# Ordering every engine's work by the program text in the merge stage of a hybrid attention/GLA step

## The chip, the cores and the metric

The kernel runs on one core of one Trainium2 chip. The metric is the device time of one execution, in microseconds, as the median of several runs. TensorE (PE in the profile) multiplies, VectorE (DVE), ScalarE (ACT) and GpSimd (POOL) work on tiles, and SyncE (SP) issues the transfers of the stage that this document is about.

## The reference

One inference step over 2048 new prompt tokens and 64 sample tokens (2112 in all), model width 1024. Sliding-window attention and gated linear attention (GLA) run beside each other; their outputs are projected, gated per channel, added, projected again and normalised with the residual. The part that matters here is the end:

```python
h_att = jnp.einsum('bta,ad->btd', o_att * jax.nn.silu(g_att), w_pa)
h_gla = jnp.einsum('btv,vd->btd', o_gla * jax.nn.silu(g_gla), w_pg)
merged = jax.nn.sigmoid(r_att) * h_att + jax.nn.sigmoid(r_gla) * h_gla
y = jnp.einsum('btd,de->bte', merged, w_o)
x = layer_norm(DN_ALPHA * x + y, ln_g, ln_b)
```

`r_att` and `r_gla` are projections of x (weights `w_ra` and `w_rg`), so there are four large products of the tokens with a weight matrix, then one with `w_o`. Everything is float32.

## The kernel before

**Stages.** First the attention over six token chunks, then the GLA over four heads times six chunks, then the merge (lines 970 to 1144), then the output projection with the normalisation (line 1149 on). All of it is one program without loops on the chip.

**Precision.** Each float32 operand is split in two parts: `split` (lines 111 to 114) copies it on ACT with rounding (`xh`, `wh`) and takes the rest on DVE (`xl`, `wl`). A product is three matmuls: hi*hi, hi*lo, lo*hi (lines 1141 to 1143).

**The merge.** It has four *passes*: pass 0 with `w_pa` on the attention's output, pass 1 with `w_ra` on x, pass 2 with `w_rg` on x, pass 3 with `w_pg` on the GLA's output. Each pass multiplies in blocks by a Strassen-like scheme with seven products, in the *steps* 1, 2, 7, 6, 5, 3, 4 (`ORDER`). Each step runs over three token parts (`MS`), so a pass has 21 *units* (n, counted from 0 to 83), and each unit has four *groups*, one for each output block p. A group is 6 matmuls in pass 0 and 12 in the others, of 352 columns each, into one PSUM bank. There are five such banks (`pa`), and a group can start when the bank of the group five before it has been read.

**What follows a group.** `combine` reads the bank. Steps 1 and 7 copy it with ACT (lines 1025 and 1031). Step 6 adds on DVE (L1034) and then on POOL (L1035). Steps 2, 5, 3 and 4 complete an output block: they add on DVE (L1028, L1038 with L1039, L1042, L1045) and call the pass's *sink*. Pass 0 stores the block (L1051). Pass 1 takes a tanh on ACT (L1054), a multiply with a loaded block `cs` on DVE (L1055), and stores (L1056). Pass 2 takes a tanh on ACT (L1059) and stores (L1060). Pass 3 multiplies with a loaded block on DVE (L1063), adds another on POOL (L1064) and stores (L1065).

**What goes ahead of a unit.** The input block of unit n+2 (n+3 in pass 0) is loaded (L1001), that of unit n+1 is split, the raw weight tiles `ws` of a later step are loaded (L975), added on POOL for the steps that need sums (lines 982 to 988), and split into `wh` and `wl`. The weights of a step are made over the three units before it: two blocks in the first, one in each of the other two. There are two buffers for split inputs, so the input of unit n+1 can be split only when PE has finished unit n-1. The blocks `cs` are loaded four groups ahead into eight buffers. Blocks that end in the `fin` tile (steps 2 and 5) share six buffers.

**Besides.** In pass 2 the last six *input sums* (`combine_x`, loads L831 and L832, POOL lines 834 to 837, stores L839) prepare inputs for pass 3. In pass 3 four of the eight tiles of `w_o` are loaded (L1105) and split, for the stage behind the merge.

**What sets the order.** PE's instructions run in the order of the text throughout (a `manual_schedule` region for PE). For the other engines and SP's queue of transfers a planner places each instruction, by its own estimate of when it can start and with text order as priority. An engine executes its queue in that order: an instruction that waits holds up all behind it. The planner can thus put an instruction far ahead of its place in the text; in this kernel the first `w_o` load, which the text has in unit 64, stands in SP's queue while PE is in unit 33.

Of the kernel before, what the change touches and what calls it, by code (L numbers as in the profile page):

```python
# [51 lines left out]
def kernel(ctx, tc, io):  # L52
# [773 lines left out]

    def combine_x(new):
# [9 lines left out]
        nc.gpsimd.tensor_tensor(x2[:, t0], x1[:, t0], x2[:, t0], ALU.subtract)  # L837
        for n_, x_, t in ((0, x1, t1), (1, x1, t0), (2, x2, t1), (3, x2, t0)):
            nc.sync.dma_start(dst[n_, :, s, k], x_[:, t])  # L839

    def chain(B):
# [117 lines left out]
    def toks(s, t):  # L959
        return slice((2 * s + t) * T, (2 * s + t + 1) * T)  # L960

    class Pass:

        def __init__(self, w, kh, src, kept, parts, sink):
            self.w, self.kh, self.src, self.kept, self.parts, self.sink = w, kh, src, kept, parts, sink
            self.A, self.acc = {}, {}
# [9 lines left out]

        def prep_w(self, i, p, r):
            A, tt = self.A, nc.gpsimd.tensor_tensor  # L980
            if i == 7:
                tt(r[0], r[0], r[1], ALU.subtract)
# [6 lines left out]
            a = A[p, "s2"] if i == 6 else A.pop((p, "s1")) if i == 5 else r[0]  # L989
# [30 lines left out]
        def combine(self, i, p, s, ps, parts):  # L1020
# [25 lines left out]
            if z is not None:  # L1046
                c, t = FINAL[i]
                self.sink(z, parts, 2 * p + c, toks(s, t))

    def store_sink(z, parts, ct, ts):  # L1050
        nc.sync.dma_start(ha_d[:, ct, ts], z)  # L1051

    def gated_sink(z, parts, ct, ts):
        nc.scalar.activation(z, z, AF.Tanh, scale=0.5)  # L1054
        nc.vector.scalar_tensor_tensor(z, z, 1.0, parts[0], ALU.add, ALU.mult)  # L1055
        nc.sync.dma_start(ta_d[:, ct, ts], z)  # L1056

    def gate_sink(z, parts, ct, ts):
        nc.scalar.activation(z, z, AF.Tanh, scale=0.5)  # L1059
        nc.sync.dma_start(tg_d[:, ct, ts], z)  # L1060

    def merge_sink(z, parts, ct, ts):
        nc.vector.scalar_tensor_tensor(z, parts[0], 1.0, z, ALU.add, ALU.mult)  # L1063
        nc.gpsimd.tensor_tensor(z, z, parts[1], ALU.add)  # L1064
        nc.sync.dma_start(mg_d[:, ct, ts], z)  # L1065

# [35 lines left out]

    def wo_load(pool, i, bufs):
        st = pool.tile([P, D], F32, tag="wst", name="wst", bufs=2)
        nc.sync.dma_start(st, io["w_o"][i])  # L1105
        hi, lo = (pool.tile([P, D], F32R, tag="wo", name=n, bufs=bufs) for n in ("woh", "wol"))
# [10 lines left out]
    issue_x(2)  # L1117
    make_x(0)
    make_w(-1)
    issue_w(0)  # L1120
    wo = []
    for n, (q, i, s) in enumerate(units):
        if n >= 2 * len(ORDER) * MS and n % 3 == 0 and combos:
            combine_x(lambda t: mtile("xc", 2 * T, 5))
        if n >= 3 * len(ORDER) * MS and n % 4 == 0 and len(wo) < 4:
            wo.append(wo_load(mo, len(wo), 8))
        issue_x(n + 3 if q.kh == 2 else n + 2)
        issue_w(n + 1)
        make_x(n + 1)
        make_w(n)  # L1130
        xh, xl = xp.pop(n)
        for p in range(NP4):
# [6 lines left out]
            for k in range(q.kh):  # L1139
# [3 lines left out]
                mm(ps, wl[:, ks], xh[:, ts], start=False, stop=(k == q.kh - 1))  # L1143
            q.combine(i, p, s, ps, parts.get(g))
    phase.close()
# [5 lines left out]
    for i in range(len(wo), 8):  # L1151
        wo.append(wo_load(sb, i, 8))
    wo = [wo[:4], wo[4:]]
# [162 lines left out]
```

## Time and profile before

| | |
|---|---|
| median of 3 runs | 1909.57 us (1908.79 to 1911.14) |
| the profiled execution | 1904.76 us |
| its span, first to last instruction | 1902.9 us |
| PE busy | 1819.0 us, 96% |
| DVE, ACT, POOL busy | 1243.9, 847.8, 518.2 us |
| granted clock of PE, mean | 0.983 |
| merge, first to last matmul | 1095.87 to 1687.70 us |

The profile is one execution; times in it are microseconds from the span's first instruction. "L1055" is line 1055 of the kernel. A row of the timeline has start, duration, engine, line, operation, what it writes and reads, and in brackets how long its engine was idle before it and what ended that. A row of a group has `xcount | total busy, mean ns | idle before it`, with the releasers. A row of the waits has the total, the number and the longest.

### The profile page before, as it was taken

Reading aid. Unit: us, or ns where it says so; the run is one execution under the profiler, and the core shown is the slowest. Engines: PE = TensorE matmul, PEld = TensorE weight load, DVE = VectorE, ACT = ScalarE, POOL = GpSimd, SP = SyncE. Lnnn points to the kernel's source line nnn. Section 1 sums busy time; section 2 is a strip of 40 time slices with the busy share of each in tenths; the row PEclk is TensorE's granted clock in tenths of the full one; section 3 lists DMA queues with packets and bytes.
Section 4 is the critical chain, followed back from the end, with each engine's and each line's share of the span. In section 5 each row is a group of like instructions: output and inputs, shape, how many; then the busy total and the mean of one; then the engine's idle time right before and its main releaser. Section 6 shows DMA issues by size and latency. Waiting matters only on the chain.

```text
span 1902.9 us, 32427 instructions
## 1 busy us (share of the span) xinstructions
PE 1819.0 (96%) x11683; PEld 1725.1 (91%) x11683; DVE 1243.9 (65%) x2552; ACT 847.8 (45%) x1942; POOL 518.2 (27%) x667
## 2 busy tenths in 40 slices
PE   6999999999999999999999799997999999979997
PEld 5988998889999999999999799997999999967886
DVE  4587768755675666557655559648746655956665
ACT  3444546545664664556555453434553543221100
POOL 3310111422134114213321133552322154621121
PEclk8999999999999999999999999998999999989999
DMA  6211012543365236424722289878975866884441
GB/s 223 89 38 41 25 45 86 157 144 115 106 216 179 84 122 227 146 81 147 227 79 61 78 278 309 284 268 297 322 238 169 261 216 214 272 296 168 137 138 60
DMA packets 200929, 316.03 MB, mean 166 GB/s; under 512 B 21720, under 2 KB 162864, under 8 KB 200752
## 3 DMA queue, kind: packets, MB, share of 16 engines
q1 hardware_dynamic: 195520, 307.70, 49.5%
q0 software_dynamic: 5248, 6.26, 1.2%
q8 instruction: 92, 1.51, 0.3%
q14 instruction: 69, 0.57, 0.1%
HBM read 228.72 MB, written 86.14 MB: 165 GB/s over the span
## 4 chain that ended last, share of the span: by engine, by line
PE 77%; DMA 8%; DVE 5%; POOL 4%; ACT 3%; issue 2%; SPq 1%; POOLq 0%; DVEq 0%; ACTq 0%
PE pd L180 9%; PE pd L181 9%; PE pd L182 9%; PE pa L1142 7%; PE pa L1141 7%; PE pa L1143 7%; PE pd L193 6%; PE pd L195 6%; PE pd L194 6%; PE pa L401 2%; DMA wst<-w_o 1%; DMA cs<-tg_d 1%; PE pa L386 1%; PE pa L731 1%; PE pa L732 1%
## 5 line engine op out<-in xcount | busy, mean ns | idle before, releaser
L180 PE MATMUL pd<-x,wh 128*128 128x384 f32 (+2 forms) x1248 | 409.6, 328 | 8.4 <-ACT x L113 5.3
L182 PE MATMUL pd<-x,wl 128*128 128x384 f32 (+2 forms) x1248 | 403.6, 323 | 1.3 <-DVE wl L114 1.3
L181 PE MATMUL pd<-x,wh 128*128 128x384 f32 (+2 forms) x1248 | 403.8, 324 | 0.9 <-DVE x L114 0.9
L1141 PE MATMUL pa<-xh,wh 128*128 128x352 f32 x1176 | 382.7, 325 | 17.7 <-DVE a L1034 9.7
L1142 PE MATMUL pa<-xl,wh 128*128 128x352 f32 x1176 | 380.6, 324 | 7.6 <-DVE xl L114 7.3
L1143 PE MATMUL pa<-xh,wl 128*128 128x352 f32 x1176 | 379.8, 323 | 0.0
L180 PEld LDWEIGHTS pd<-x,wh 128*128 128x128 f32 x1248 | 236.8, 190 | 17.8 <-issue 8.1
L1141 PEld LDWEIGHTS pa<-xh,wh 128*128 128x128 f32 x1176 | 222.2, 189 | 19.6 <-DVE a L1034 10.0
L181 PEld LDWEIGHTS pd<-x,wh 128*128 128x128 f32 x1248 | 236.8, 190 | 2.3 <-DVE x L114 2.1
L182 PEld LDWEIGHTS pd<-x,wl 128*128 128x128 f32 x1248 | 236.3, 189 | 1.9 <-DVE wl L114 1.9
L1142 PEld LDWEIGHTS pa<-xl,wh 128*128 128x128 f32 x1176 | 223.2, 190 | 11.9 <-DVE xl L114 11.8
L1143 PEld LDWEIGHTS pa<-xh,wl 128*128 128x128 f32 x1176 | 221.9, 189 | 0.0
L114 DVE TENSOR_TENSOR xl<-xs,xh 128x1408 fp32r<-128x1408 f32 x63 | 108.0, 1714 | 75.9 <-ACT xh L113 61.8
L113 ACT CAST x<-xst 128x384 fp32r<-128x384 f32 (+3 forms) x164 | 77.9, 485 | 160.2 <-PE pd L194 121.4
L193 PE MATMUL pd<-wh,x 128*128 128x256 f32 x512 | 148.0, 289 | 0.0
L194 PE MATMUL pd<-wh,x 128*128 128x256 f32 x512 | 144.9, 283 | 0.3 <-POOL x L114 0.2
L195 PE MATMUL pd<-wl,x 128*128 128x256 f32 x512 | 144.6, 282 | 0.0
L113 ACT CAST xh<-xs 128x1408 fp32r<-128x1408 f32 x63 | 86.4, 1372 | 99.5 <-PE pa L1143 75.4
L723 POOL TENSOR_SCALAR sq<-sq 128x1 f32<-128x1 f32 (+1 forms) x68 | 17.8, 262 | 375.3 <-ACT ring L722 375.3
L193 PE MATMUL pd<-woh,x 128*128 128x512 f32 x256 | 101.8, 398 | 13.2 <-ACT x L113 9.8
L194 PE MATMUL pd<-woh,x 128*128 128x512 f32 x256 | 101.3, 396 | 0.9 <-DVE x L114 0.9
L195 PE MATMUL pd<-wol,x 128*128 128x512 f32 x256 | 101.3, 396 | 0.6 <-DVE wol L114 0.5
(310 smaller groups left out, 3753.1 us busy)
## 6 DMA issues: line engine op xcount, KB each, us to landing
wst<-wt SPq DMA_DIRECT2D x33, 512.0 KB, 3.6
xs<-xc_d SPq DMA_DIRECT2D x24, 704.0 KB, 5.5
u<-xT SPq DMA_DIRECT2D x84, 192.0 KB, 3.9
xst<-xT SPq DMA_DIRECT2D x76, 192.0 KB, 2.7
xs<-xT SPq DMA_DIRECT2D x18, 704.0 KB, 6.1
ws<-w_ra SPq DMA_DIRECT2D x36, 256.0 KB, 4.7
ws<-w_rg SPq DMA_DIRECT2D x36, 256.0 KB, 5.1
ws<-w_pg SPq DMA_DIRECT2D x36, 256.0 KB, 3.9
```

The costliest lines, as they stand in the source:

```text
L113: nc.scalar.copy(dst_h, src)
L114: eng.tensor_tensor(dst_l, src, dst_h.bitcast(F32), ALU.subtract)
L180: mm(ps, hi[:, s], xh[:, :T], start=(k == 0), stop=False)
L181: mm(ps, hi[:, s], xl[:, :T], start=False, stop=False)
L182: mm(ps, lo[:, s], xh[:, :T], start=False, stop=(k == n - 1))
L193: mm(ps, xh[:, xs], hi, start=(k == 0), stop=False)
L194: mm(ps, xl[:, xs], hi, start=False, stop=False)
L195: mm(ps, xh[:, xs], lo, start=False, stop=(k == KT - 1))
L401: mm(ot[pr, :], vb[:, pr], A["pT", bi, kv][:, hf], start=(hf == h0), stop=(hf == 1))
L1141: mm(ps, wh[:, ks], xh[:, ts], start=(k == 0), stop=False)
L1142: mm(ps, wh[:, ks], xl[:, ts], start=False, stop=False)
L1143: mm(ps, wl[:, ks], xh[:, ts], start=False, stop=(k == q.kh - 1))
```

## The change

All other engines are put under a `manual_schedule` region too, from the first instruction of the merge to its last, so that in the merge ACT, DVE, POOL and SP also run in the order of the text. The text is rearranged for it. The making of a weight tile is divided into its sum (`sum_w`, POOL, at the start of a unit) and its split (`prep_w`, ACT and DVE, after the unit's first group). A sink returns its store instead of issuing it; the store is issued two groups later (at once in the last unit). An input sum is divided into its loads (at unit n), its sums on POOL (in unit n+2, after the third group) and its stores (in unit n+3). A `w_o` tile is loaded at units 69, 73, 77 and 81 and split two units later, after the third group. Loads now stand ahead of input sums and `w_o` in a unit. What is computed stays the same.

```diff
         x1, x2 = new("x1")[:, :2 * MT], new("x2")[:, :2 * MT]
         nc.sync.dma_start(x1, src[:, k, ts])
         nc.sync.dma_start(x2, src[:, kh + k, ts])
+        return dst, k, s, x1, x2
+
+    def combine_sums(c):
+        x1, x2 = c[3:]
...
     def gated_sink(z, parts, ct, ts):
         nc.scalar.activation(z, z, AF.Tanh, scale=0.5)
         nc.vector.scalar_tensor_tensor(z, z, 1.0, parts[0], ALU.add, ALU.mult)
-        nc.sync.dma_start(ta_d[:, ct, ts], z)
+        return lambda: nc.sync.dma_start(ta_d[:, ct, ts], z)
...
+    def add_w(n):
+        for u, q, i, p in plan.get(n, []):
+            raws[u, p] = q.sum_w(i, p, raws.pop((u, p)))
+
     def make_w(n):
         for u, q, i, p in plan.get(n, []):
-            wts[u, p] = q.prep_w(i, p, raws.pop((u, p)))
+            wts[u, p] = q.prep_w(raws.pop((u, p)))
...
+    ET = mybir.EngineType
+    phase.enter_context(tc.manual_schedule(engines={ET.Activation, ET.DVE, ET.Pool, ET.SP}))
+    wo, later, stores = [], {}, deque()
+
+    def at_unit(n, fn):
+        later.setdefault(n, []).append(fn)
+
+    def flush(n):
+        while len(stores) > n:
+            fn = stores.popleft()
+            if fn is not None:
+                fn()
...
+    U = len(ORDER) * MS
     for n, (q, i, s) in enumerate(units):
-        if n >= 2 * len(ORDER) * MS and n % 3 == 0 and combos:
-            combine_x(lambda t: mtile("xc", 2 * T, 5))
-        if n >= 3 * len(ORDER) * MS and n % 4 == 0 and len(wo) < 4:
-            wo.append(wo_load(mo, len(wo), 8))
         issue_x(n + 3 if q.kh == 2 else n + 2)
         issue_w(n + 1)
+        if n >= 2 * U and n % 3 == 0 and combos:
+            c = combine_load(lambda t: mtile("xc", 2 * T, 5))
+            at_unit(n + 2, lambda c=c: combine_sums(c))
+            at_unit(n + 3, lambda c=c: combine_store(c))
+        if n >= 3 * U + 4 and n % 4 == 1 and len(wo) < 4:
+            st = wo_load(mo, len(wo))
+            wo.append(None)
+            at_unit(n + 2, lambda st=st, j=len(wo) - 1: wo.__setitem__(j, wo_split(mo, st, 8)))
         make_x(n + 1)
-        make_w(n)
+        add_w(n)
...
-            q.combine(i, p, s, ps, parts.get(g))
+            stores.append(q.combine(i, p, s, ps, parts.get(g)))
+            flush(0 if n == len(units) - 1 else 2)
+            if p == 0:
+                make_w(n)
+            if p == 2:
+                for fn in later.pop(n, []):
+                    fn()
```

More of the change, by code (lines that the diff above doesn't have):

```diff
@@ L825, with combine_load @@
                    [(ug_d, uc_d, 4, k, s) for k0 in (0, 2) for s in range(MS) for k in (k0, k0 + 1)])
-    def combine_x(new):
+    def combine_load(new):
         src, dst, kh, k, s = combos.popleft()
@@ L837, in combine_x, with combine_store @@
         nc.gpsimd.tensor_tensor(x2[:, t0], x1[:, t0], x2[:, t0], ALU.subtract)
+    def combine_store(c):
+        dst, k, s, x1, x2 = c
+        t0, t1 = slice(0, MT), slice(MT, 2 * MT)
         for n_, x_, t in ((0, x1, t1), (1, x1, t0), (2, x2, t1), (3, x2, t0)):
             nc.sync.dma_start(dst[n_, :, s, k], x_[:, t])
+    def combine_x(new):
+        c = combine_load(new)
+        combine_sums(c)
+        combine_store(c)
     def chain(B):
@@ L1047, in combine @@
                 c, t = FINAL[i]
-                self.sink(z, parts, 2 * p + c, toks(s, t))
+                return self.sink(z, parts, 2 * p + c, toks(s, t))
     def store_sink(z, parts, ct, ts):
-        nc.sync.dma_start(ha_d[:, ct, ts], z)
+        return lambda: nc.sync.dma_start(ha_d[:, ct, ts], z)
     def gated_sink(z, parts, ct, ts):
@@ L1064, in merge_sink @@
         nc.gpsimd.tensor_tensor(z, z, parts[1], ALU.add)
-        nc.sync.dma_start(mg_d[:, ct, ts], z)
+        return lambda: nc.sync.dma_start(mg_d[:, ct, ts], z)
     passes = [Pass(io["w_pa"], 2, ua_d, ac_d, [], store_sink),
```

17 lines of the change are left out of this document (10 added, 7 removed).

## The prediction

> **What bounds the kernel now.** I read the page first, then the busy times over stretches cut at the first matmul of each of the merge's four passes, then PE's waits, then the timeline at the longest wait.
>
> ```profile
> span 1902.9 us, 32427 instructions
> ...
> PE 1819.0 (96%) x11683; PEld 1725.1 (91%) x11683; DVE 1243.9 (65%) x2552; ACT 847.8 (45%) x1942; POOL 518.2 (27%) x667
> ```
>
> PE is busy 96% of the span, so no other engine's work counts unless PE waits for it. Columns of the next view: stretch, its length, PE busy (instructions), granted clock, DMA share, GB/s.
>
> ```profile
> 1088.47:1095.87 7.40, 0.23 (x2) 0.77 0.92 290
> 1095.87:1182.94 87.07, 84.97 (x505) 0.98 0.90 295
> 1182.94:1363.10 180.16, 166.29 (x1011) 0.96 0.87 290
> 1363.10:1523.26 160.16, 160.16 (x1011) 1.00 0.72 233
> 1523.26:1687.70 164.44, 162.28 (x1010) 1.00 0.75 243
> 1687.70:1720.00 32.30, 17.70 (x53) 0.74 0.81 278
> ```
>
> Rows two to five are passes 0 to 3. By the code pass 0 has 504 matmuls and the others 1008 each (the rows count those at the edges too). Pass 2 never waits: 160.16/1008 = 0.1589 us a matmul, 7.63 us a unit of 48, 1.91 us a group of 12. At that rate the passes would take 80.1, 160.2, 160.2 and 160.2; they lose 7.0, 20.0, 0 and 4.2 us. **These 31 us are all that the change can win in the merge.** PE's waits there:
>
> ```profile
> PE pa L1141 <- DVE a L1034: 9.7, 1, 9.7
> PE pa L1142 <- DVE xl L114: 7.3, 7, 2.2
> PE pa L1141 <- ACT wh L113: 7.2, 1, 7.2
> ```
>
> The third is the start, in the row 1088.47. The first is this:
>
> ```profile
> 1283.44 1.23 SPq L1105 DMA_DIRECT2D wst<-w_o  x2
> 1289.87 1.04 ACT L113 CAST woh<-wst 128x1024 fp32r<-128x1024 f32 x1 [15.44 <-DMA wst<-w_o]
> 1290.95 1.78 DVE L114 TENSOR_TENSOR wol<-wst,woh 128x1024 fp32r<-128x1024 f32 x1 [15.01 <-ACT woh L113]
> 1292.65 0.51 DVE L1034 TENSOR_TENSOR a<-a,pa 128x352 f32<-128x352 f32 x1
> 1293.22 0.66 PE L1141 MATMUL pa<-xh,wh 128*128 128x352 f32 x1 [9.68 <-DVE a L1034]
> ```
>
> A w_o split, which the text has in pass 3, was put into ACT's and DVE's queues in pass 1, ahead of its own load. Both engines stood 15 us behind it; the adds that free PSUM came late; PE ran out of banks.
>
> **The change, part by part.** *Start.* The first x, four weights, x, x and two weights are issued in the same order as now: 0. From 1 us better to 1 us worse (one row of start-up DMAs holds 7.4 us).
>
> *w_o and late input sums.* Now issued from 1283 on; in the text w_o comes at units 69, 73, 77 and 81, with its split two units (15 us) after the load, and the last six input sums come in pass 2, whose DMA share is 0.72. The 9.7 us wait and its slow restart go.
>
> *Pass 0.* DVE's items there:
>
> ```profile
> L114 DVE TENSOR_TENSOR xl<-xc,xh 128x704 fp32r<-128x704 f32 x21 | 20.0, 953 | 14.4 <-ACT xh L113 13.4 <-DMA ws<-w_pa 1.0
> L1038 DVE TENSOR_TENSOR fin<-a,pa 128x352 f32<-128x352 f32 x48 | 24.6, 513 | 4.2 <-issue 2.6 <-PE pa L1143 1.5
> L1039 DVE TENSOR_TENSOR a<-a,pa 128x352 f32<-128x352 f32 x48 | 24.6, 512 | 0.0
> ```
>
> A unit of step 5 costs xl 0.9, eight adds at 0.44 start to start and 0.6 of weight splits: about 5.0 against PE's 3.81. Three such units put DVE 3.5 us behind, of which the five banks hide all but some 1.2. The slow restart at the beginning (1.8 of the 7.0) stays. So 80.1 + 1.8 + 1.2 = 83.1, **4.0 saved**; between 5.1 (all hidden) and 0 (PE waits as now).
>
> *Pass 1, the new wait.* Its sink is an add (DVE), a tanh (ACT) and a multiply (DVE) on one tile. In the order of the text DVE can start nothing between add and multiply, except in step 5 its second add. Behind the waiting multiply stand the weight splits, the next group's add (it frees a PSUM bank for PE) and the xl of the next unit but one; behind ACT's tanh stands that unit's xh. Each piece is in these rows:
>
> ```profile
> 1348.56 0.51 DVE L1045 TENSOR_TENSOR a<-a,pa 128x352 f32<-128x352 f32 x1
> 1349.63 0.52 DVE L1055 SCALAR_TENSOR_TENSOR a<-a,cs 128x352 f32<-128x352 f32 x1 [0.56 <-ACT a L1054]
> 1350.08 0.52 DVE L1045 TENSOR_TENSOR a<-a,pa 128x352 f32<-128x352 f32 x1
> 1350.90 1.63 DVE L114 TENSOR_TENSOR xl<-xs,xh 128x1408 fp32r<-128x1408 f32 x1 [0.30 <-ACT xh L113]
> 1352.44 1.62 DVE L1055 SCALAR_TENSOR_TENSOR a<-a,cs 128x352 f32<-128x352 f32 x1
> ...
> 1349.11 0.50 ACT L1054 ACTIVATE a<-a 128x352 f32<-128x352 f32 x1 [1.03 <-DVE a L1045]
> 1349.51 1.36 ACT L113 CAST xh<-xs 128x1408 fp32r<-128x1408 f32 x1
> ```
>
> Add to next add is 1.52 us. Now I walk one unit that is limited this way, from the end D of the previous unit's last multiply. Its tanh began at D-1.04; xh follows at D-0.64 and ends at D+0.72; xl runs from D+0.75 to D+2.38, and DVE goes on at D+2.29. One group: D+3.81. One weight split (0.60 start to start, 0.06 waiting for wh): D+4.47. Three groups: D+9.10. With two splits (the first unit of a step) D+9.70. The mean is 9.3 us, against PE's 7.63.
>
> Now unit by unit, with PE at 0 at the first unit of step 5 and no arrears: the next unit's xl ends at 3.1, so D is 10.4, then 19.5, 28.6, 38.3, 47.4, 56.5, 66.2, 75.3, 84.4. PE may start a unit 2.38 after the D of the last but one: the first four start on time, the next seven (the last of them is pass 2's second unit) wait 0.5, 2.1, 1.5, 1.5, 2.1, 1.5 and 1.5, 10.7 us. Step 2 has three such units and loses 0.5. POOL can lengthen this: the multiply at 1352.44 took 1.62 instead of 0.52 beside this add:
>
> ```profile
> 1351.44 2.23 POOL L982 TENSOR_TENSOR ws<-ws 128x512 f32<-128x512 f32 x1 [15.33 <-ACT a L1054]
> ```
>
> Four such adds fall into the nine units; each can cost 1.1, I take 2.5 in all. The Trainium skill (SBUF — State Buffer, "SBUF: two separate sides") says that a DVE instruction with two SBUF inputs and a GpSimd instruction exclude each other for a whole instruction. By that rule any of the four that starts first blocks the multiply, 4.4 us; the two rows agree.
>
> Pass 1: 160.2 + 10.7 + 0.5 + 2.5 = 173.9, **6.3 saved** of the 20.0. The low bound is 160.2. For the high one the rows' means hold instead of their undisturbed values:
>
> ```profile
> L114 DVE TENSOR_TENSOR xl<-xs,xh 128x1408 fp32r<-128x1408 f32 x63 | 108.0, 1714 | 75.9 <-ACT xh L113 61.8 <-PE pa L1142 7.4 <-DMA xc<-ug_d 6.6
> L114 DVE TENSOR_TENSOR wl<-ws,wh 128x512 fp32r<-128x512 f32 x84 | 71.8, 863 | 11.5 <-ACT wh L113 11.2
> L1055 DVE SCALAR_TENSOR_TENSOR fin<-fin,cs 128x352 f32<-128x352 f32 x24 | 16.9, 711 | 4.6 <-ACT fin L1054 4.3
> ```
>
> That adds 4 x 0.19, 0.09 and 1.33 x 0.17 to a unit, 10.4 us in all; nine units lose 20 and step 2 another 4: 184.
>
> *Pass 2.* Its sink ends with the tanh, and DVE doesn't wait for it. From the last add: xh 0.44 later, xl to 3.4, an add, tanh and wh to 5.0, a split, three adds: 6.9 us, 8.2 in step 5, for three units only. The banks hide that: 0.
>
> *Pass 3.* DVE waits for no engine, only for the two loads of each group.
>
> ```profile
> 1617.03:1687.70 70.67, 69.95 (x433) 69.36 (x432) 59.84 (x93) 13.91 (x13) 40.08 (x35) 1.00 0.88 281
> 1660.00:1670.00 10.00, 10.00 (x64) 10.00 (x63) 7.34 (x10) 1.37 (x1) 6.05 (x5) 1.00 1.01 345
> ...
> ws<-w_pg SPq DMA_DIRECT2D x36, 256.0 KB, 3.9
> cs<-tg_d SPq DMA_DIRECT2D x48, 176.0 KB, 3.9
> mg_d<-fin SPq DMA_DIRECT2D x24, 176.0 KB, 3.7
> wst<-w_o SPq DMA_DIRECT2D x4, 512.0 KB, 5.8
> ```
>
> The last nine units (first row, with DVE busy 59.84 us) move 281 GB/s x 70.67 = 19.9 MB now. In the text's order five weight tiles (1.3 MB), two w_o loads (1.0) and an x (0.7) come on top: 3.0 MB, 8.9 us at the 345 GB/s of a full DMA. Against it stand the 12% of share that are free (8.5 us) and the loads' lead of four groups. I take 2.5 us of waiting, bounds 0 and 8.9: 160.2 + 0.3 + 2.5 = 163.0, **1.4 saved**. The Trainium skill (DMA: Bandwidth & Descriptors, "Specifications") puts a core's share of HBM at about 358 GB/s; by it the 22.9 MB take an estimated 64 us, less than nine units of 7.63, and the term would be near 0.
>
> *Stores two groups later.* They reach SP's queue behind two groups' loads and so wait less there. The cover is the fin tile's reuse after six groups: in pass 0 that is 5.7 us, for an add, an issue and a landing of together about 5. If that is late, pass 0 goes to its upper bound.
>
> *PE's two speeds.* After some waits PE runs slightly slower, with nothing waiting:
>
> ```profile
> 1380.00:1420.00 40.00, 40.00 (x254) 40.00 (x253) 20.84 (x26) 20.93 (x35) 9.63 (x7) 1.00 0.81 264
> 1580.00:1620.00 40.00, 40.00 (x250) 40.00 (x250) 20.61 (x26) 14.76 (x21) 16.23 (x13) 1.00 0.54 183
> ```
>
> That is at most 1.6%. Which speed follows pass 1's last wait I can't tell: 0 to 4.8 us over passes 2 and 3, I take half, 2.4 **lost**.
>
> *Handover.* The row 1687.70:1720.00 has 14.6 us without PE, behind the last stores and the loads of the next stage; neither is moved: 0, from -3 to 3.
>
> **Sum.** -4.0 - 6.3 - 1.4 + 2.4 = -9.3 us. The profiled execution took 1904.76 us (span 1902.9 and 1.9 around it), so 1895.5 for one like it. It lies 4.8 below the median of the runs, 1909.57; against that median I predict 1900 us.
>
> **Rivals.** *Everything flows* (0.14): the scheduler's detours were all, and multiply, tanh and add hide behind PSUM's five banks. For it: pass 2 runs without a wait. Against: 9.3 us a unit is over 7.63 for nine units in a row. Passes 0, 1 and 3 save 5, 20 and 4: 1881.
>
> *The tail is bound by transfers* (0.14): share 1.01 at 345 GB/s is all there is, and the 8.9 us come in full; with pass 1's POOL adds at their dearest the gain is down to 1: 1908.5. Against it: a share of only 0.88 over that stretch.
>
> *Pass 1's chain costs more than the detours did* (0.12; slower). One mechanism: the period of its limited units. Each 1 us on it costs 12 us (nine units and three). My 9.3 and the POOL adds equal 9.5; at 10.3 the whole gain is gone, and at 10.8 it is 1916. For it: the means give 10.4. Against: they hold POOL's interference from passes in which POOL has far more to do.
>
> *The order was near the text already* (0.06): 1909.5. Against it speaks the w_o row at 1283, in unit 33 of 84.
>
> **How the numbers follow.** The forecast has 0.54, its own range is 1893 to 1906 (pass 1 between 170 and 180, the speeds either way). This kernel's measurement tells 0.2%, 3.8 us, from no change: below 1905.8 is faster, above 1913.4 slower. Faster: 0.14 and all but 0.02 of the forecast, 0.66. Same: that 0.02, 0.12 of the tail's 0.14, 0.06: 0.20. Slower: 0.12 and the rest of the tail, 0.14. The range 1886 to 1913 leaves out most of the first rival and the slower one.
>
> **What would show it.** Right: no w_o transfer before the third pass ends; in pass 1's steps 5, 3 and 4 DVE's multiply idle about 0.56 before each start behind the tanh, PE's waits of 1.5 to 2.1 us once a unit, and that pass near 174 us; pass 2 without a wait from its third unit on; pass 0 near 83. Wrong: pass 1 near 160, or above 181; more than 5 us of PE waits in pass 3; a wait of ACT for a raw weight that stops PE.

## The result, and the profile after

The change made the kernel slower: 1926.92 us (median of 4 runs, 1925.05 to 1929.97) against 1909.18 us for the kernel before on the same chip, a ratio of 1.0100 with the 95% interval 1.0072 to 1.0128. I had predicted 1900 us and a range up to 1913.

The page of the kernel after:

```profile
span 1923.5 us, 32300 instructions
...
PE 1828.9 (95%) x11683; PEld 1729.9 (90%) x11683; DVE 1242.0 (65%) x2552; ACT 845.0 (44%) x1942; POOL 515.6 (27%) x667
```

Every engine runs as many instructions as before (PE 11683, DVE 2552, ACT 1942, POOL 667), and DVE, ACT and POOL are busy 2 to 3 us less. No work was added. In the four passes PE is idle 13.7 us more than before, and it is busy 5.7 us longer with the same matmuls, which run slower behind a stall (the rows below show a granted clock of 0.80 in unit 13 and 0.89 in unit 70, against 1.00 in passes 1 and 2). The next view cuts the run at the first matmul of each pass, as in the prediction (length, busy us of PE, PEld, DVE, ACT, POOL, granted clock, DMA share, GB/s):

```profile
1098.46:1191.18 92.72, 85.87 (x504) 83.14 (x505) 64.93 (x121) 36.92 (x75) 25.61 (x28) 0.96 0.70 228
1191.18:1363.98 172.80, 163.53 (x1010) 160.54 (x1009) 110.84 (x166) 73.95 (x117) 37.60 (x28) 1.00 0.73 243
1363.98:1529.42 165.44, 162.16 (x1010) 160.25 (x1009) 96.17 (x129) 75.72 (x123) 66.60 (x52) 1.00 0.76 259
1529.42:1709.70 180.28, 167.87 (x1010) 164.85 (x1008) 122.98 (x168) 55.07 (x75) 93.70 (x74) 0.97 0.81 273
```

| stretch | before | predicted | after |
|---|---|---|---|
| span start to first matmul of the merge | 1095.87 | same | 1098.46 |
| pass 0 | 87.07 | 83.1 | 92.72 |
| pass 1 | 180.16 | 173.9 | 172.80 |
| pass 2 | 160.16 | 160.2 | 165.44 |
| pass 3 | 164.44 | 163.0 | 180.28 |
| end of pass 3 to span end | 215.2 | same | 213.8 |

Pass 1 came as predicted. Passes 0, 2 and 3 lose what it wins and 19 us more. Where inside them: cut at the first matmuls of single units, the stretches that are longer than PE's own 3.81 us (pass 0) or 7.63 us a unit are these. The rows are unit 13; unit 20; units 36 to 43; unit 70; units 77 to 82.

```profile
1151.94:1160.63 8.69, 5.50 (x26) 5.21 (x25) 5.52 (x12) 1.80 (x4) 4.06 (x6) 0.80 0.33 101
1184.46:1191.18 6.72, 4.08 (x26) 3.80 (x25) 3.22 (x6) 1.88 (x2) 0.00 (x0) 1.00 1.05 360
1307.81:1382.14 74.33, 64.26 (x384) 61.55 (x385) 50.91 (x81) 32.99 (x55) 3.32 (x4) 1.00 0.85 278
...
1582.81:1598.13 15.32, 9.74 (x51) 9.17 (x49) 7.56 (x6) 5.15 (x10) 12.71 (x9) 0.89 0.92 337
1643.89:1701.83 57.94, 51.14 (x291) 48.98 (x289) 46.64 (x71) 13.45 (x14) 33.68 (x27) 0.94 1.00 332
```

They lose 4.9, 2.9, 13.3, 7.7 and 12.2 us (length less 3.81 or 7.63 for each unit). What is behind each?

**Unit 13.** The timeline of POOL, ACT and DVE:

```profile
1141.47 12.30 POOL L1051 TENSOR_TENSOR a<-a,a 128x352 f32<-128x352 f32 x11 [0.86 <-DVE a L1050]
1153.73 2.27 POOL L1002 TENSOR_TENSOR ws<-ws 128x256 f32<-128x256 f32 x3
...
1154.49 0.41 ACT L113 CAST wh<-ws 128x256 fp32r<-128x256 f32 x1 [5.38 <-POOL ws L1002]
...
1154.93 0.49 DVE L114 TENSOR_TENSOR wl<-ws,wh 128x256 fp32r<-128x256 f32 x1 [3.80 <-ACT wh L113]
1156.21 0.51 DVE L1054 TENSOR_TENSOR fin<-a,pa 128x352 f32<-128x352 f32 x1
```

In the text the weight sums of step 3 (L1002) stand behind step 6's adds. One such add takes POOL 1.12 us (12.30/11), a group only 0.95 us on PE (3.81/4), so POOL is behind its twelve groups when step 6 ends. ACT stands 5.38 us at a split of the weight that is not summed yet, DVE 3.80 us behind ACT, and DVE's adds that free PSUM's banks (L1054) come behind that. PE stops.

**Unit 20.** SP, ACT, DVE and PE:

```profile
1179.63 0.56 SPq L989 DMA_DIRECT2D ws<-w_ra  x1
...
1187.34 0.62 ACT L113 CAST wh<-ws 128x512 fp32r<-128x512 f32 x1 [5.42 <-DMA ws<-w_ra]
...
1187.99 0.69 DVE L114 TENSOR_TENSOR wl<-ws,wh 128x512 fp32r<-128x512 f32 x1 [3.50 <-ACT wh L113]
...
1189.17 0.43 PE L1185 MATMUL pa<-xh,wh 128*128 128x352 f32 x1 [2.63 <-DVE a L1061]
```

This is the same queue with a load at its head. A raw weight of pass 1 lands 7.7 us after its request, and the DMA share is 1.05 in this unit. ACT's split stands 5.42 us for it, DVE 3.50 us behind ACT, and behind that stands the add (L1061) that frees the bank PE waits for.

**Units 36 to 43.** DVE and ACT at the first of them:

```profile
1305.45 0.51 DVE L1054 TENSOR_TENSOR fin<-a,pa 128x352 f32<-128x352 f32 x1
1305.88 0.52 DVE L1055 TENSOR_TENSOR a<-a,pa 128x352 f32<-128x352 f32 x1
1306.53 0.53 DVE L1071 SCALAR_TENSOR_TENSOR fin<-fin,cs 128x352 f32<-128x352 f32 x1
1307.79 1.62 DVE L114 TENSOR_TENSOR xl<-xs,xh 128x1408 fp32r<-128x1408 f32 x1 [0.74 <-ACT xh L113]
...
1305.99 0.50 ACT L1070 ACTIVATE fin<-fin 128x352 f32<-128x352 f32 x1 [1.02 <-DVE fin L1054]
1306.40 1.36 ACT L113 CAST xh<-xs 128x1408 fp32r<-128x1408 f32 x1
```

This is the predicted ping-pong: tanh behind add, multiply behind tanh, xh behind tanh, xl behind xh. The eight units take 74.33/8 = 9.29 us each; the prediction's walk gave 9.3.

**Unit 70.** SP, DVE, POOL and ACT:

```profile
1572.87 3.87 SPq L989 DMA_DIRECT2D ws<-w_pg  x6
1576.84 0.39 SPq L1032 DMA_DIRECT2D cs<-tg_d  x1
...
1583.21 0.53 DVE L1079 SCALAR_TENSOR_TENSOR fin<-cs,fin 128x352 f32<-128x352 f32 x1 [3.17 <-DMA cs<-tg_d]
...
1583.87 2.19 POOL L1080 TENSOR_TENSOR fin<-fin,cs 128x352 f32<-128x352 f32 x1 [3.18 <-DMA mg_d<-fin]
1586.03 1.28 POOL L998 TENSOR_TENSOR ws<-ws 128x512 f32<-128x512 f32 x1
1587.39 1.29 POOL L999 TENSOR_TENSOR ws<-ws 128x512 f32<-128x512 f32 x1
...
1588.72 0.62 ACT L113 CAST wh<-ws 128x512 fp32r<-128x512 f32 x1 [8.37 <-POOL ws L999]
```

Six weight tiles were asked for ahead of a block `cs`; the block lands 6.4 us after its request, DVE's multiply waits 3.17 us for it, POOL's add comes behind the multiply (its row names a store, but the multiply had ended 0.13 us before), two weight sums behind the add, ACT's split behind the sums (8.37 us idle), and behind the split ACT's copies that free PSUM. PE waits twice in this unit: 2.19 us for the xl behind that multiply, and 3.38 us for one of the copies.

**Units 77 to 82.** DMA share 1.00. Waits of DVE and of ACT from 1643 to 1702 us:

```profile
DVE a L1079 <- DMA cs<-tg_d: 6.9, 4, 2.4
DVE fin L1079 <- DMA cs<-tg_d: 1.4, 1, 1.4
...
ACT wh L113 <- POOL ws L1002: 12.6, 2, 8.1
```

DVE's multiplies stand 8.3 us for blocks that land late; in kernel 8 below, which loads fewer of them, DVE stands 1.3 us. ACT's splits also wait for POOL's sums here, and they do so in kernel 8 (15.3 us).

### The profile page after: what moved, and what is told of

Its sections match the earlier page's. It is cut to its first block, busy times and chain, and to the rows that moved or that the text cites. A ratio compares the mean times of both kernels' runs of the same rounds, so it can differ in the third digit from the quotient of the medians.

```text
span 1923.5 us, 32300 instructions
## 1 busy us (share of the span) xinstructions
PE 1828.9 (95%) x11683; PEld 1729.9 (90%) x11683; DVE 1242.0 (65%) x2552; ACT 845.0 (44%) x1942; POOL 515.6 (27%) x667
## 5 line engine op out<-in xcount | busy, mean ns | idle before, releaser
L114 DVE TENSOR_TENSOR wl<-ws,wh 128x512 fp32r<-128x512 f32 (+1 forms) x112 | 83.8, 764 | 51.2 <-ACT wh L113 50.8
```

What stands on the lines that cost most here:

```text
L114: eng.tensor_tensor(dst_l, src, dst_h.bitcast(F32), ALU.subtract)
```

## The experiments

Ratios are against the kernel before run in the same job; its own median was 1905.83 us in the job of the first four, then 1905.63, 1904.89 and 1903.49. So I compare ratios between jobs and not times; 0.001 is 1.9 us. The length of one pass scatters between runs of the same text: pass 1 took 172.80, 175.74, 174.91 and 173.14 us in the kernel after and in three kernels below that differ from it only later. Single stalls scatter too: with the same text there, unit 70 lost 7.7 us in the kernel after and 5.3 and 8.5 in kernels 4 and 8 (7.9 in kernel 11, where only a load of w_o is missing ahead of it), and units 77 to 82 lost 12.2, and 8.9 and 9.7 in kernels 4 and 13. So pass lengths within 3 us of each other (4 in pass 3) are the same, and the whole time decides where it can. Pass 3 is given to the end of its last matmul in the first row and to that matmul's start in the others, 0.3 us less.

| kernel | us | ratio (95%) | pass 0 | 1 | 2 | 3 |
|---|---|---|---|---|---|---|
| after | 1926.9 | 1.0100 (1.0072–1.0128) | 92.7 | 172.8 | 165.4 | 180.3 |
| 1 new text, planned | 1897.3 | 0.9957 (0.9936–0.9977) | 85.4 | 174.3 | 161.3 | 163.6 |
| 2 old text, in order | 1984.5 | 1.0408 (1.0382–1.0434) | 99.1 | 180.4 | 195.0 | 199.1 |
| 3 splits a unit later | 1930.0 | 1.0128 (1.0107–1.0149) | 86.5 | 180.6 | 168.0 | 183.1 |
| 4 multiply a group later | 1911.2 | 1.0023 (1.0009–1.0036) | 91.4 | 165.0 | 163.3 | 176.0 |
| 5 SP alone in order | 1902.3 | 0.9982 (0.9969–0.9995) | 87.0 | 164.5 | 163.6 | 172.2 |
| 6 ACT, DVE, POOL in order | 1919.4 | 1.0080 (1.0063–1.0098) | 87.2 | 175.9 | 168.1 | 174.7 |
| 7 sums a unit earlier | 1913.8 | 1.0050 (1.0032–1.0068) | 84.7 | 175.3 | 163.1 | 175.9 |
| 8 less loaded, last steps | 1916.9 | 1.0064 (1.0047–1.0081) | 93.6 | 175.7 | 165.2 | 175.1 |
| 9 SP in order, w_o early | 1902.1 | 0.9986 (0.9973–1.0000) | 86.8 | 164.6 | 165.9 | 171.3 |
| 10 three mends | 1898.8 | 0.9962 (0.9945–0.9979) | 85.5 | 164.1 | 165.2 | 175.7 |
| 11 w_o early | 1927.5 | 1.0112 (1.0092–1.0132) | 93.5 | 174.9 | 169.2 | 175.3 |
| 12 stores at once | 1938.6 | 1.0171 (1.0150–1.0191) | 94.9 | 178.2 | 167.1 | 183.0 |
| 13 less loaded, step 2 | 1922.7 | 1.0089 (1.0059–1.0120) | 93.1 | 173.1 | 165.5 | 176.8 |
| 14 requests spread | 1898.4 | 0.9959 (0.9939–0.9979) | 85.6 | 163.5 | 165.1 | 167.8 |
| 15 three mends, planned | 1885.9 | 0.9905 (0.9873–0.9936) | 84.9 | 167.5 | 162.4 | 161.9 |

### Text and order apart (1 and 2)

The change does two things: it rearranges the text, and it makes four engines follow it. Kernel 1 is the new text without the fixed order:

```diff
-    phase.enter_context(tc.manual_schedule(engines={ET.Activation, ET.DVE, ET.Pool, ET.SP}))
```

> The changed kernel without the region that orders ACT, DVE, POOL and SP: the new text, placed by the planner. Theory (the fixed order of four queues costs it: waits behind unready instructions in pass 0 at unit 13, in pass 3 at unit 70 and in pass 3's last nine units): the 17.7 us go back, 1905 to 1912 us, units 13 and 70 without a wait over 1 us. Rival (the rearranged text itself costs it: later stores, w_o and weights loaded into pass 3's busy end): 1920 to 1930, and pass 3's last nine units still take 80 us.

Kernel 2 is the old text with it:

```diff
+    ET = mybir.EngineType
+    phase.enter_context(tc.manual_schedule(engines={ET.Activation, ET.DVE, ET.Pool, ET.SP}))
     issue_x(0)
     issue_w(-1)
```

> The kernel before with the region alone: the old text, all engines in its order. Theory (in a fixed order every instruction placed ahead of what it needs stops its queue): input sums whose stores stand right behind their sums hold SP some 10 us each, six times, and a w_o split right behind its load holds ACT and DVE some 6 us each, four times: 1945 to 1975 us. Rival (the order of the text is much the same as the planner's, and the placing of splits, sums and stores matters little): within 8 us of the changed kernel, 1919 to 1935.

Measured: 0.9957 and 1.0408. The times, 1897.3 and 1984.5 us, lie 8 us below the range of the first theory and 10 us above that of the second. **The new text by itself makes the kernel faster by 0.4%; the fixed order costs 1.4% with it, and 4.1% with the old text.** The rearranging was worth some 58 us under a fixed order, and still it was not enough. In kernel 2 SP stands some 60 us at stores of input sums and ACT 29.7 us at w_o splits, as the theory had it; what each cost PE was not tried apart. What the planner does better is seen where unit 13 stood. POOL in kernel 1:

```profile
1139.54 0.74 POOL L1002 TENSOR_TENSOR ws<-ws 128x256 f32<-128x256 f32 x1 [0.25 <-DMA ws<-w_pa]
1140.24 12.69 POOL L1051 TENSOR_TENSOR a<-a,a 128x352 f32<-128x352 f32 x11
```

The last of step 3's four weight sums, too, is placed ahead of the eleven adds; unit 13 loses 1.2 us instead of 4.9. The cost of the planner's freedom shows in the same kernel in unit 34 (19.11 us instead of 7.63), where it had put a w_o load into pass 1, as in the kernel before:

```profile
1296.58 1.04 ACT L113 CAST woh<-wst 128x1024 fp32r<-128x1024 f32 x1 [18.14 <-DMA wst<-w_o]
...
1284.12:1303.23 19.11, 9.22 (x51) 8.94 (x49) 5.18 (x9) 4.93 (x7) 6.42 (x8) 0.73 0.79 269
1627.62:1674.02 46.40, 46.40 (x290) 46.40 (x289) 39.24 (x57) 10.64 (x10) 27.35 (x22) 1.00 0.96 312
```

ACT stands 18.14 us for that load. The last row is its units 77 to 82: a loss of 0.6 us, at 312 GB/s.

### Which engine's order (5 and 6)

```diff
-engines={ET.Activation, ET.DVE, ET.Pool, ET.SP}
+engines={ET.SP}
```

> The changed text with only SyncE's instructions (the requests of transfers) held in the order of the text; ScalarE, VectorE and GpSimd are ordered by the planner. Without any fixed order the same text took 1897.3 us, 11.5 us of which were one stall at unit 34, where the planner had put input-sum stores and an output-weight load into pass 1. Theory: what costs time is the fixed order of the computing engines (a split that stands ahead of copies that would free PSUM), and SyncE's order is not harmful in itself. Then the passes before the last come as in the planned kernel, unit 34's stall is gone, and the time is 1885 to 1892 us. Rival: the fixed order's loss is mostly in the transfers (the output-weight loads and the depth of two stores collide in the last pass). Then units 77 to 82 still lose about 12 us, and the time is 1898 to 1912 us.

```diff
-engines={ET.Activation, ET.DVE, ET.Pool, ET.SP}
+engines={ET.Activation, ET.DVE, ET.Pool}
```

> The reverse: ScalarE, VectorE and GpSimd in the order of the text, SyncE ordered by the planner. Theory (the computing engines' order costs): units 13, 20, 70 and 36 to 43 lose what they lose in the changed kernel, about 4.9, 2.9, 7.7 and 13.5 us, and the time is 1910 to 1930 us. Rival (SyncE's order costs): the time comes near the fully planned 1897 us.

Against the planned 0.9957, SP's order alone costs 0.0025 (4.8 us), that of the three engines alone 0.0123 (23 us); together 28 us, and all four cost 0.0143 (27 us). So the two about add up (each ratio is uncertain by some 0.002), and **some five sixths come from the order of the computing engines.** Kernel 6 lies in its theory's range; units 13, 70 and 36 to 43 lose 3.9, 5.8 and 17.7 us there, and unit 20 nothing. My theory for SP alone had 1885 to 1892, and was wrong by 10 us: unit 34's stall did go (first row), but the tail lost 6.9 us of it again (second row, units 77 to 82, 45.8 us without waits). The time lies in the rival's range, though the rival had about 12 us for these units.

```profile
1284.50:1292.24 7.74, 7.74 (x51) 7.74 (x50) 5.17 (x9) 2.78 (x4) 1.30 (x1) 1.00 0.91 290
1623.35:1676.02 52.67, 48.63 (x291) 47.51 (x289) 41.45 (x61) 11.90 (x13) 27.34 (x22) 0.97 1.00 340
```

### The single heads of queues (3, 4 and 7)

Kernel 3 makes a split one unit later, so that its sum is there:

```diff
-            if p == 0:
-                make_w(n)
+            if p == 0 and n:
+                make_w(n - 1)
```

> The changed kernel with each weight split one unit later in the text (behind the first group of the following unit), so that POOL has a unit more for its sum. Theory (the waits at units 7 to 9, 13, 28 and 70 are ACT's and DVE's queues standing at a weight split whose POOL sum is late): these four waits, 1.7 + 4.8 + 1.7 + 7.7 us, fall to 3 together: 1912 to 1918 us. Rival (it is the transfers of the raw weights or of the inputs that are late, and the split only shows it): less than 4 us gained, 1923 to 1930.

Pass 0 fell by 6.2 us, but the time didn't: the last of a step's four weights is now split in the unit that multiplies with it. Its time is the rival's, but not for the rival's reason, late transfers. PE's waits in the merge name the new head:

```profile
PE pa L1185 <- ACT wh L113: 21.3, 8, 6.9
PE pa L1187 <- DVE wl L114: 18.5, 10, 5.0
```

Kernel 4 takes pass 1's multiply out of the way; it is issued behind the addition of the next group:

```diff
-        nc.vector.scalar_tensor_tensor(z, z, 1.0, parts[0], ALU.add, ALU.mult)
+        mults.append(lambda: nc.vector.scalar_tensor_tensor(z, z, 1.0, parts[0], ALU.add, ALU.mult))
...
+            old, mults[:] = mults[:], []
             stores.append(q.combine(i, p, s, ps, parts.get(g)))
+            for fn in old:
+                fn()
```

> The changed kernel with pass 1's multiply placed behind the next group's add, so that the tanh runs meanwhile. Theory (in pass 1 DVE stands 0.56 us at each multiply and xl one tanh later, 9.3 us a unit): the waits of units 35 to 43, 13.5 us by the count of matmuls, fall under 2: 1913 to 1917 us, pass 1 at 162 us. Rival (DVE is bound there by its own work or by POOL's lock, not by the tanh): under 4 us gained, 1922 to 1930.

Pass 1 fell from 172.8 to 165.0, and units 36 to 43 from 74.33 to 65.25 us:

```profile
1303.39:1368.64 65.25, 63.15 (x385) 61.19 (x385) 48.18 (x82) 32.95 (x55) 1.42 (x1) 1.00 0.93 306
...
1307.04 0.52 DVE L1073 SCALAR_TENSOR_TENSOR fin<-fin,cs 128x352 f32<-128x352 f32 x1
1307.47 0.52 DVE L1054 TENSOR_TENSOR fin<-a,pa 128x352 f32<-128x352 f32 x1
1307.91 0.52 DVE L1055 TENSOR_TENSOR a<-a,pa 128x352 f32<-128x352 f32 x1
1308.34 0.52 DVE L1073 SCALAR_TENSOR_TENSOR fin<-fin,cs 128x352 f32<-128x352 f32 x1
```

Multiply and adds now follow each other every 0.43 us without a wait for the tanh. That shows the ping-pong as the cause of 9.1 of the 13.3 us in these units (the theory had all but 2 of them). 4.2 us stay. PE's only waits left there are for xl (2.1 us): it stands behind xh, and xh still stands behind the tanh. The ratio fell by 0.0077, 15 us; 9 of them are in these units, and the rest lies in passes whose text is the same, within what such passes scatter.

Kernel 7 loads and sums the weights a unit earlier, and leaves the splits where they are:

```diff
-        issue_w(n + 1)
+        issue_w(n + 2)
...
-        add_w(n)
+        add_w(n + 1)
```

> The changed kernel with weights loaded and summed one unit earlier (loads for unit n+2 asked for and sums for unit n+1 made at the start of unit n; the splits stay behind group 0 of unit n). Theory: unit 13 lost 4.9 us because GpSimd's eleven adds of step 6 stood ahead of the sum that a split on ScalarE waited for, with PSUM's copies behind it; with sums a unit ahead the split finds its operand ready. Unit 13 falls to under 1 us, unit 70 (7.7 us, the same with a late transfer) to under 3, unit 28 (1.7) to under 1, and the time by 8 to 12 us to 1915 to 1919 us. Rival: the sum itself isn't late but ScalarE's order is (the split has to be run anyhow between copies), or the sums, now issued earlier, only stand ahead of the adds of step 6 and delay those: then unit 13 keeps over 3 us and the time stays within 4 us of 1927.

As the theory had it: unit 13 lost nothing (3.87 us), pass 0 fell to 84.7, and the ratio by 0.0050, 10 us. So **POOL's place for the sums, not the split, was late in pass 0.** Unit 70 kept 5.3 us, more than expected and no less than it scatters. Unit 28 kept its 1.7 us, where the theory had under 1: in the kernel after PE waits 1.43 us there for an xl behind the multiplies of pass 1's step 2, and kernel 4, which moves the multiplies, loses nothing there.

### The transfers (8, 9, 11, 12 to 14)

Kernel 8 loads one block instead of two in the last three steps of pass 3:

```diff
-            for d in self.parts:
+            for j, d in enumerate(self.parts):
+                if j and i != 2:
+                    out.append(out[0])
+                    continue
                 y = mtile("cs", T, 8)
```

> The changed kernel without the loads of the second block (ta) in the last three steps of pass 3: the first block is added in its place, so what is computed there is not the reference's. It leaves out 3 steps x 2 halves... of 4 blocks each of 180 KB, about 4.3 MB at most of the 24.7 MB moved between 1617 and 1710 us, at about 345 GB/s some 12 us of transfers. Theory: units 77 to 82 of the changed kernel (12.2 us lost) wait for transfers at a rate that is spent; with less to move they lose under 3 us, and the time falls by 9 to 12 us to 1915 to 1918 us. Rival: they wait for the order of the engines (a VectorE instruction that stands ahead of PSUM's copies whatever its transfer does): the losses stay above 8 us and the time above 1922 us.

Units 77 to 82 lose 5.1 us here, where the kernels with this text that load all lose 8.9 to 12.2, and the ratio fell by 0.0036, 7 us. The time is in the theory's range, the 5.1 us lie between the theory's 3 and the rival's 8. So 4 to 7 us of the tail are transfers; about 5 stay with a DMA share of 0.89, and 14.6 MB moved instead of 19.2. What these 5 are was not tried.

Kernels 11 (the kernel after) and 9 (SP alone in order) ask for w_o in pass 2:

```diff
-        if n >= 3 * U + 4 and n % 4 == 1 and len(wo) < 4:
+        if n >= 2 * U + 1 and n % 4 == 1 and len(wo) < 4:
```

> The changed kernel with the output-weight loads in units 45, 49, 53 and 57 and nothing else. Theory: the tail's transfers run at a spent rate (share 0.99 to 1.02, about 340 GB/s, from 1650 us on); without the two loads of units 77 and 81, 1.05 MB or 3.1 us at 340 GB/s, units 77 to 82 lose 8 to 9 us instead of 11.6, and unit 70 up to 1.5 us less (the load of unit 69); the time falls by 3 to 5 us to 1922 to 1924 us. Rival: the splits of the output weights on ScalarE and VectorE, which the order sets in between, are what disturbs, and they now disturb pass 2: pass 2 rises by as much and the time stays within 2 us of 1927.

> Only SyncE in the order of the text, and the four output-weight loads (0.5 MB each) asked for in units 45, 49, 53 and 57 of pass 2 instead of units 69, 73, 77 and 81 of pass 3. With SyncE alone in order the time was 1902.3 us, and units 79 to 82 lost 6.5 us at a DMA share of 0.99. Theory: that loss is transfers at a spent rate; two of the four loads, 1.05 MB, leave the stretch from 1630 us on, at 335 GB/s 3.1 us of it, so units 79 to 82 lose 2 to 4 us and the time is 1897 to 1900 us. Rival: the loss is the place of the requests in SyncE's queue (input slabs asked for two units ahead behind stores), not the rate: then 79 to 82 keep 6 us or more and the time stays above 1901 us.

In both the tail's units got shorter (57.94 to 52.67, and 52.67 to 48.99 us), and in neither did the time move: pass 2 grew by 3.8 and 2.2 us. A single profile can't tell the latter from scatter, but the ratios can tell that nothing was won (1.0112 and 0.9986 against 1.0100 and 0.9982). Kernel 11 came as its rival had it: units 56 and 57, with a w_o split on ACT at 1481.19, lose 5.0 us, where the kernel after loses 1.0. Kernel 9 lost 3.1 us in units 79 to 82, as its theory had it, but its time is the rival's.

Kernel 12 issues each store right behind its group:

```diff
-            flush(0 if n == len(units) - 1 else 2)
+            flush(0)
```

> The changed kernel with each store issued right behind its group instead of two groups later. A store of pass 1 waits for tanh and multiply, of pass 3 for the addition on GpSimd, and SyncE's later requests stand behind it. Theory: SyncE would stand at every store for the 3 to 4 us of that chain, but the requests are for units ahead, so only the short leads suffer (second blocks and slabs in the tail): pass 3 grows by 3 to 10 us and the time is 1930 to 1937 us. Rival: SyncE's queue has slack everywhere, and the delay of two groups bought nothing, or costs because the buffers come free later: 1920 to 1928 us.

Slower by another 0.0071, 13 us: **the delay of the stores by two groups is worth some 13 us**, and the place isn't the one I expected. Pass 1 grew by 5.4 us, pass 3 only by 3.0; the largest single rise is unit 28 (14.25 us instead of 9.3), where SP's and DVE's queues show why:

```profile
1242.99 0.47 SPq L1032 DMA_DIRECT2D cs<-ha_d  x1
1245.33 5.99 SPq L1072 DMA_DIRECT2D ta_d<-fin  x4
...
1250.11 0.86 DVE L1071 SCALAR_TENSOR_TENSOR fin<-fin,cs 128x352 f32<-128x352 f32 x1 [3.71 <-ACT wh L113]
```

With stores between the requests, SP asks for the block `cs` of unit 26's last group 10.2 us after that unit began; in the kernel after it is 7.3 us. The block lands 7.0 us later, and the multiply waits 3.71 us for it (the row names ACT, but the tanh before this multiply had ended 3 us earlier). Behind the multiply stand the xl for which PE waits 4.94 us, and the last of the four stores at which SP stands 5.99 us.

What unit 70 waits for was still open. Kernel 13 leaves out the second block in step 2 of pass 3 alone, ahead of unit 70:

```diff
-            for d in self.parts:
+            for j, d in enumerate(self.parts):
+                if j and i == 2:
+                    out.append(out[0])
+                    continue
                 y = mtile("cs", T, 8)
```

> The changed kernel without the loads of the second block (ta) in step 2 of pass 3 (the first block is added in its place, so the merged rows of that step are not the reference's): 12 loads of 180 KB, 2.16 MB less between about 1540 and 1585 us, where the DMA share is 1.02 at 366 GB/s. Theory A: unit 70's 7.6 us begin with transfers at a spent rate (the first block came 3.2 us late for VectorE, the sums then late for ScalarE's split); 2.16 MB are 5.9 us at 366 GB/s, so unit 70 loses under 2.5 us and the time falls by 5 to 8 us to 1919 to 1922 us. Theory B: unit 70 loses it in the order (GpSimd's additions and weight sums one after the other, ScalarE's split ahead of PSUM's copies), whatever the transfers do: then unit 70 keeps over 5 us and the time is above 1924 us.

Kernel 10 puts the mends of 4, 7 and 11 together, and kernel 14 spreads its weight requests:

> All engines in the order of the text, with three mends: pass 1's multiply behind the next group's addition (alone 15.8 us faster than the changed kernel), weights loaded and summed a unit earlier (alone 13.1 us faster), output-weight loads in pass 2 (not run alone). Theory: the losses are separate heads of queues, so the gains add: pass 0 at 85, pass 1 at 165, pass 2 at 162, pass 3 at 172 to 175 us, and the time is 1895 to 1900 us, faster than before by 5 to 14 us. Rival: a fixed order hands the stall on to the next head of a queue, as it did when the splits were put a unit later (1930.0 us): then less than half of the summed gains comes, and the time is above 1906 us.

```diff
-        issue_w(n + 2)
...
+            if p in (0, 2):
+                issue_w(n + 2, p // 2, p // 2 + 1)
             if p == 0:
                 make_w(n)
```

> The kernel with three mends (1898.8 us, unit 70 loses 5.7 us of it) with the weight requests of a unit put behind its groups 0 and 2 instead of all six tiles (1.5 MB) ahead of the unit's blocks. Theory A (transfers in a burst): the blocks that VectorE waited 3.3 to 3.6 us for stood behind six tiles, 1.57 MB or 4.4 us at 355 GB/s; with three ahead of them at a time they come about 2.2 us earlier, unit 70 loses 2 to 4 us, and the time is 1895 to 1898 us. Theory B (the order of the engines): unit 70 keeps its 5.7 us, and the sums of weights that come later put new stalls into units 27, 28 and 69: 1900 to 1906 us.

Unit 70 in kernels 13, 10 and 14, one row each (7.63 us without waits):

```profile
1584.04:1596.80 12.76, 9.40 (x51) 9.11 (x49) 5.51 (x4) 5.24 (x10) 11.80 (x9) 0.87 0.92 328
```

```profile
1565.19:1578.65 13.46, 10.33 (x49) 10.09 (x49) 8.90 (x6) 5.44 (x11) 10.89 (x7) 0.75 0.91 318
```

```profile
1566.48:1575.99 9.51, 8.02 (x50) 7.78 (x49) 7.32 (x6) 5.24 (x11) 7.71 (x4) 1.00 0.97 350
```

With 2.16 MB less to load, unit 70 still loses 5.1 us, which is inside its scatter, and ACT's split waits 8.5 us for POOL's sums as before: theory B by the bounds set, though the time lies between the two theories. (The share of 1.02 that the expectation gives is that of 1570 to 1590 us; from 1540 to 1585 it is 0.82.) Kernels 5 and 6 say the same: with SP's order alone unit 70 loses 0.1 us, with the computing engines' order alone 5.8. So **the stall of unit 70 needs the fixed order of the computing engines**: with the requests in the same order and these engines planned, it is gone. But it is not mended by one step. With the sums a unit earlier (kernel 10) ACT's splits no longer wait, and the unit loses 5.8 us to a slab of x and to blocks that land late, behind weight tiles. With these requests spread (kernel 14) it loses 1.9. One late operand stood behind the other, and **taking one away shows the next.** The whole time of kernel 14 can't be told from kernel 10's (0.9959 against 0.9962), though pass 3 was 7.9 us shorter in its profile: 10 runs lie between 1893.55 and 1901.51, and the profiled one is the fastest.

Kernel 10's gains added up: 0.0077 and 0.0050 from the single mends and none from w_o, 0.0138 together (26 us); its theory had 1895 to 1900. The fixed order, mended, is as fast as the planned new text, and faster than the kernel before by 0.2 to 0.6%.

### Mends and planner together (15)

Kernel 15 is kernel 10 without the fixed order, the same line taken out as in kernel 1.

> The three mends in the text, with all engines but TensorE ordered by the planner. The planned changed text took 1897.3 us, of which unit 34 lost 11.4, as the planner had put output-weight loads and input-sum stores into pass 1. Theory: the planner orders by its own costs, not by the text, so the mends move little, unit 34's stall stays, and the time is 1893 to 1900 us. Rival: the multiply that is written behind the next group takes the wait from VectorE in the planner's order too, and the stall at unit 34 goes: 1883 to 1890 us, the fastest of all.

Its units 34 and 35, and its units 77 to 82:

```profile
1283.17:1301.75 18.58, 16.21 (x99) 15.44 (x97) 16.77 (x29) 8.31 (x14) 8.65 (x8) 1.00 0.91 291
...
1618.88:1664.96 46.08, 46.08 (x290) 46.08 (x289) 40.74 (x58) 10.64 (x10) 26.04 (x22) 1.00 0.98 322
```

The rival was right: unit 34's stall is gone (two units lose 3.3 us together instead of 12 in kernel 1), although w_o is still loaded in pass 1, and the tail loses almost nothing. **1885.85 us, ratio 0.9905 (0.9873 to 0.9936): faster than both kernels.** Which of the three mends took the stall away was not tried apart.

## Why the prediction was wrong

The prediction gave 1895.5 us for an execution like the profiled one; the profiled one of the kernel after took 1925.3. The 29.8 us between them are +9.6 in pass 0, -1.1 in pass 1, +5.2 in pass 2, +17.3 in pass 3, +2.6 ahead of the merge, -1.4 behind it, and -2.4 for PE's slower speed, which did not come.

**Pass 0: the step that failed.** I costed DVE's arrears (3.5 us, hidden but for 1.2) and held PE's waits for that. POOL's queue I never walked, though the fixed order covers it and the weight sums are moved past twelve adds in it. The pass took 9.6 us more than predicted, of which units 13 and 20 hold 7.8; kernel 7 takes 8 of them away (84.7). Unit 20's part is a raw weight that lands late, at the head of ACT's queue; kernels 3, 6 and 7 lose nothing there.

**Pass 1: the mechanism was right, the closeness in part luck.** 172.8 against 173.9. The old stall went. The limited units took 9.29 us against 9.3; eight of them lost 13.3 us where I had seven and 10.7, the first of them 1.6 where I had 0.5. Step 2 cost 1.7 us (unit 28) against 0.5. Against that the POOL adds, costed at 2.5, cost nothing: the four weight sums fall into units 33 to 35, which lose 0.2 us, and POOL's 3.32 us in units 36 to 43 are an input sum in the last of them.

**Pass 2: too low by 5.2 us.** 2.9 of it are units 42 and 43, which the prediction booked with pass 1 (the two passes together: 334.1 predicted, 338.2 measured). The rest includes some 2 us in units 55 to 59, where I took the chain of add, tanh, xh and xl for hidden by the banks. There ACT stands 3.04 us at a weight split (1465.73) for POOL's sum and DVE 3.80 us behind it, and the chain doesn't make up for that; in kernel 7, with the sums a unit earlier, these units lose nothing. So it is pass 0's step again.

**Pass 3: the step that failed most, 17.3 us.** Two terms. *Unit 70* (7.7 us) wasn't in the sum at all. The prediction said that DVE waits for no engine in pass 3, only for loads, and stopped there; behind such a load stood POOL's sums and ACT's split, in an order that could no longer be changed. *The tail* was taken at 2.5 us, bounds 0 and 8.9, and lost 12.2 (8.9 and 9.7 in kernels 4 and 13). The amount to be moved was right: 22.9 MB predicted for the last nine units. The view of these nine in the kernel after:

```profile
1628.64:1709.70 81.06, 74.23 (x433) 71.78 (x432) 67.88 (x100) 18.34 (x19) 49.92 (x39) 0.96 0.87 286
```

That is 286 GB/s x 81.06 us = 23.2 MB. But I averaged it over nine units. 332 GB/s x 57.94 us = 19.2 MB of it move in the six units 77 to 82, and at 7.63 us a unit that would need 420 GB/s. The free share I set against it lies outside the burst: the other three units have 4.0 MB. By kernel 8 the transfers are 4 to 7 us of the 12.2; about 5 are something else, which stays open. The Trainium skill (DMA: Bandwidth & Descriptors, "Specifications") gives a core about 358 GB/s of HBM, and I noted that by it the term would be near 0. By the same figure 19.2 MB take an estimated 54 us against 46 without waits, 8 of the 12.2 us lost: the figure, set against the right stretch, would have shown a loss, where I had set it against the wrong one. The measured rate was 332 GB/s there.

**Speeds, start, handover.** PE ran at 7.63 us a unit wherever it didn't wait, so the 2.4 us did not come. The handover gave 1.4 us, inside its bounds. The merge began 2.6 us later; first matmuls of the merge lie between 1095.65 and 1100.83 in all kernels here, so that is scatter.

**Rivals.** The tail bound by transfers (0.14) is part of what came there: the tail lost 12.2 us against its price of 8.9, and 4 to 7 of them are transfers. The slower rival named pass 1's chain, the one part that went as forecast. None had the place that decided in passes 0 and 3: a split whose operand is late, ahead of the instructions that free PSUM. Two of the signs listed as wrong were this: over 5 us of PE waits in pass 3, and ACT waiting for a raw weight until PE stops.

## What to carry to other kernels

When a planner's order is replaced by that of the text, walk the queue of every engine, the little used one too: for each instruction that can wait, ask what frees a bank or a buffer behind it, and how late its operand is at worst. Put a producer a whole unit ahead of its consumer, and a dependent step behind the next group's work; such a text helps the planner too, and here the two together were the best. Spread a budget of transfers over the stretch in which they are really asked for, not over the stage.

## What was not expected of the hardware

POOL needed 1.12 us for an addition of 128x352 (11 in 12.30 us) where DVE needs 0.51, so it is the slowest engine of pass 0's step 6, though it is busy only 25.61 of the pass's 92.72 us. At a full DMA share the rate wasn't one number: 332 GB/s in units 77 to 82, 350 in unit 70 of kernel 14 at a share of 0.97, 360 in unit 20 at 1.05, 366 from 1570 to 1590 us of the kernel after at 1.02.
